# Feed-forward loads pinned in written order, cache copies in quarters, squares one group later

## The chip, the cores and the metric

The kernel runs on one core of one Trainium2 chip. The metric is the device time of one execution in microseconds (us). Three runs of the kernel before gave 2788.48, 2798.10 and 2798.96 us; their median is 2798.1 us. One more execution was profiled.

## The reference, cut to what matters

One decoder layer is applied to a prompt of 2048 tokens and to 8 single sample tokens (float32, width 1024). The part that the change touches is the feed-forward block at the end, and two caches that are shifted by one row:

```
h2 = rmsnorm(x, norm2_g)                               # (2048 + 8) x 1024
x  = x + square(relu(h2 @ w_ff1)) @ w_ff2              # w_ff1 1024 x 4096, w_ff2 4096 x 1024
y  = rmsnorm(x, final_g)
sample_win_k = concat(cache_win_k, k_new)[:, -512:]    # 8 x 512 x 6 x 64, same for v
```

The first 511 rows of each sample's new cache are rows 1 to 511 of the old one: a plain copy in DRAM.

## The kernel before, in words

Before the feed-forward block the kernel does the input projection, the windowed attention, the recurrent mixer and the output projection (up to about 1281 us). Those parts are the same in both kernels, except that a few instructions of the last output-projection blocks stand in another order.

**Stages.** The tokens go in two halves (`SB`): 1024 tokens as two blocks of 512, then 1032 tokens as two blocks of 516. For each half the 4096 hidden features are done in two quarters of 2048 (`c`), and each of these has a first layer (`ph` 1, w_ff1) and a second layer (`ph` 2, w_ff2). That makes eight stages in a row: first half c0 first layer, c0 second layer, c1 first, c1 second, then the same four for the second half.

**Seven products.** Each stage is a matrix product of 2x2 blocks done with seven block products instead of eight. `PROD_A`, `PROD_B` and `PROD_C` (just ahead of `phase_c`) say which weight blocks are added for product p, which activation blocks are added, and into which output blocks the product goes. Five of the seven need a sum of two weight blocks (tiles ax and ay), five a sum of two activation blocks (bx and by, or two hidden tiles R in a second layer). The order is 5, 1, 2, 3, 6, 4, 7 in a first layer and 5, 3, 1, 2, 6, 4, 7 in a second.

**Steps.** A product is cut into four steps, so a stage has 28. A step does 24 matmuls of 512 columns in the first half (or 24 pairs of 258 columns in the second), in groups of 12 that end in one PSUM tile pf. Float32 precision comes from splitting each operand into a high and a low part: `split` writes the high part on ScalarE (ACT: ah, bh) and the difference on VectorE (DVE: al, bl), and three matmuls use the parts. In profile rows all of these have line L74, since they go through the wrapper `Pin`, so they are told apart by tile name.

**What sets the order.** While `pinned[0]` is set, everything issued through a `Pin` wrapper (`vec`, `act`, `gpp`) keeps its written order on its engine. The DMAs of `a_load` (L1404, L1410) and `b_load` (L1439) go through plain `nc.sync`: for these the scheduler picks the order on the SP queue. SP issues in order, so a DMA that waits for its buffer holds all DMAs behind it. For step s, `ahead(s)` first writes the split of the weights of step s+2, then the splits of activation units that are due, the sum of the weights of step s+3 on GpSimd (POOL), the activation sums that are due, the load of the weights of step s+4, and the activation loads that are due. Then `run_step` writes the matmuls of step s and, group by group, the additions of pf into the output blocks (`put`: DVE, or an ACT copy where the block is new).

**Buffers.** ax has three, ay two, bx two, by one; ah, al three each, bh, bl four each. pf has six tiles of one bank in the first half and three tiles of two banks in the second.

**Squares.** In a first layer a hidden block is complete after product 3, 6, 4 or 7. Right after that put, `run_step` lets ACT do relu and square in place on the block (two instructions a group, R<-R in the profile).

**Cache copies.** `cache_copies` copies 511 rows of one sample in one DMA of 766.5 KB, DRAM to DRAM, 16 in all. The loop at the end of `phase_c` takes one at the end of each product while the first half runs. Beside that, `bg` holds jobs that fetch, finish and store rows of the result, one a step (L1302 the fetch, L1543 the transposes, L1545 to L1558 the rest).

Of the kernel before, what the change touches and what calls it, by code (L numbers as in the profile page):

```python
# [12 lines left out]
AF = mybir.ActivationFunctionType  # L13
# [3 lines left out]
P = 128  # L17
# [42 lines left out]
def body(tc, I, O):  # L60
    nc = tc.nc
# [16 lines left out]
    act = Pin(nc.scalar)  # L78
# [38 lines left out]
    h2_d = [dram.tile([D, n], F32, name=f"h2{i}_d") for i, n in enumerate((1024, 1032))]  # L117
# [500 lines left out]
    def cache_copies():  # L618
        for src, dst in (("cache_win_k", "s_k"), ("cache_win_v", "s_v")):
            sv = I[src][0].rearrange("b t h e -> b t (h e)")  # L620
            ov = O[dst][0].rearrange("b t h e -> b t (h e)")
            for b in range(NB):
                tc.keep_in_program_order(nc.sync.dma_start(ov[b, 0:511], sv[b, 1:512]))
                yield
        nc.sync.dma_start(O["s_k"][0].rearrange("b t h e -> b t (h e)")[:, 511], ks_d)
        nc.sync.dma_start(O["s_v"][0][:, 511], vs_d.rearrange("b (h e) -> b h e", e=HD + 1)[:, :, :HD])
        nc.sync.dma_start(O["s_conv"][0][:, 0:2], I["state_conv"][0][:, 1:3])
        yield
# [707 lines left out]
    def phase_c(om, o):  # L1336
# [31 lines left out]
        for sb in range(2):  # L1368
            for c in range(2):
                for ph in (1, 2):  # L1370
                    for p in ORDER[ph]:
                        dsets = ((0, 1, 2, 3),) if ph == 1 or sb == 0 else ((0, 1), (2, 3))
                        nf = 2 if len(dsets) == 1 else 4
# [3 lines left out]
                        for ds in dsets:  # L1377
                            for f0 in range(0, 8, nf):
                                bs = range(base, base + 2) if ph == 1 else range(base + f0 // 2, base + (f0 + nf) // 2)
                                for b in bs:  # L1380
# [3 lines left out]
                                                  end=False))  # L1384
# [5 lines left out]
            u_["ss"] = u_["es"] - 1  # L1390
            u_["ls"] = u_["ss"] - 1
        nb_ = dict(ls=0, ss=0, es=0)
        gpp = Pin(nc.gpsimd)

        def a_load(s):
            d = steps[s]
            blocks = PROD_A[d["p"]]
            tl = []
            for (r, q), name in zip([x for x in blocks[:2] if x], ("ax", "ay")):
                x = wst.tile([P, 4 * 256], F32, name=name, bufs=3 if name == "ax" else 2)  # L1400
                if d["ph"] == 1:
                    f0 = 2048 * d["c"] + 1024 * r + P * d["fs"][0]
                    src = w1[512 * q:512 * q + 512, f0:f0 + 256].rearrange("(k p) f -> p k f", p=P)
                    nc.sync.dma_start(x.rearrange("p (k f) -> p k f", k=4), src)  # L1404
                else:
                    nf, nd = len(d["fs"]), len(d["ds"])
                    f0 = 2048 * d["c"] + 1024 * q + P * d["fs"][0]
                    c0 = 512 * r + P * d["ds"][0]
                    src = w2[f0:f0 + P * nf, c0:c0 + P * nd].rearrange("(i p) d -> p i d", p=P)
                    nc.sync.dma_start(x.rearrange("p (i d) -> p i d", i=nf), src)  # L1410
                tl.append(x)
            d["raw"] = tl

# [15 lines left out]
        def b_load(j):  # L1429
            u_ = bunits[j]  # L1430
            W = SB[u_["sb"]][1]
            blocks = [x for x in PROD_B[u_["p"]][:2] if x]
            if u_["ph"] == 2:
                return
            u_["raw"] = []
            for (kh, th), name, nb in zip(blocks, ("bx", "by"), (2, 1)):
                x = wst.tile([P, 2, 516], F32, name=name, bufs=nb)[:, :, :W]
                r0 = 512 * kh + 256 * u_["j"]
                nc.sync.dma_start(x, h2_d[u_["sb"]][r0:r0 + 256, th * W:th * W + W].rearrange("(k p) t -> p k t", p=P))  # L1439
                u_["raw"].append(x)  # L1440

        def b_sum(j):
# [18 lines left out]
        def b_stage(s, key, f):  # L1461
            while nb_[key] < len(bunits) and bunits[nb_[key]][key] <= s:
                f(nb_[key])
                nb_[key] += 1

        def a_stage(s, f):
            if 0 <= s < len(steps):
                f(s)

        def ahead(s):  # L1470
            a_stage(s + 2, a_split)
            b_stage(s, "es", b_split)
            a_stage(s + 3, a_sum)
            b_stage(s, "ss", b_sum)
            a_stage(s + 4, a_load)
            b_stage(s, "ls", b_load)

        def put(dst, src, sign, new, nb):
            if nb > 1:
                dst = dst.rearrange("p (n w) -> p n w", n=nb)  # L1480
            if new:
                act.activation(dst, src, AF.Copy, scale=float(sign))
            else:
                vec.tensor_tensor(dst, dst, src, op=OP.add if sign > 0 else OP.subtract)

        def run_step(s, pool_, acc):
            d = steps[s]
            sb, c, ph, p = d["sb"], d["c"], d["ph"], d["p"]
            _, W, nb = SB[sb]
            w = W // nb  # L1490
            ah, al = d.pop("w")
            nf = len(d["fs"])

            def group(parts):
                pf = pool_.tile([P, nb, 512], F32, name="pf1", tag="f1")
                for i, (lh, ll, bh, bl) in enumerate(parts):
                    for x_, y_, fst, lst in ((lh, bh, i == 0, False), (lh, bl, False, False), (ll, bh, False, i + 1 == len(parts))):
                        for n in range(nb):
                            pe.matmul(pf[:, n, :w], x_, y_[:, n * w:n * w + w], start=fst, stop=lst)  # L1499
                return pf[:, :, :w] if nb > 1 else pf[:, 0, :w]  # L1500

            if ph == 1:
                av = [a.rearrange("p (k f) -> p k f", k=4) for a in (ah, al)]
                bu = [bunits[d["b0"] + j]["x"] for j in range(2)]
                for i, f in enumerate(d["fs"]):
                    fs = slice(P * i, P * i + P)
                    pf = group([(av[0][:, k, fs], av[1][:, k, fs], bu[k // 2][0][:, k % 2], bu[k // 2][1][:, k % 2])
                                for k in range(4)])
                    for blk, sign in PROD_C[p]:
                        new = (blk, f // 2, i) not in first  # L1510
                        if new and (i == 0):
                            R[blk, f // 2] = rp.tile([P, 2, 516], F32, name=f"R{blk[0]}{blk[1]}{f // 2}")
                        first[blk, f // 2, i] = True
                        cv = R[blk, f // 2][:, i, :W]
                        put(cv, pf, sign, new, nb)
                        if (blk, p) in (((0, 1), 3), ((1, 0), 4), ((1, 1), 6), ((0, 0), 7)):
                            act.activation(cv, cv, AF.Relu)
                            act.activation(cv, cv, AF.Square)
            else:
                av = [a.rearrange("p (i d) -> p i d", i=nf) for a in (ah, al)]  # L1520
                for dl, dp in enumerate(d["ds"]):
                    dsl = slice(P * dl, P * dl + P)
                    if (dp, "pf") not in d["open"]:
                        d["open"][dp, "pf"] = pool_.tile([P, nb, 512], F32, name="pf1", tag="f1")
                    pf = d["open"][dp, "pf"]
                    for i, f in enumerate(d["fs"]):
                        bh, bl = bunits[d["b0"] + f // 2]["x"]
                        bh, bl = bh[:, f % 2], bl[:, f % 2]
                        for x_, y_, a, b in ((av[0], bh, f == 0, False), (av[0], bl, False, False), (av[1], bh, False, f == 7)):
                            for n in range(nb):  # L1530
                                pe.matmul(pf[:, n, :w], x_[:, i, dsl], y_[:, n * w:n * w + w], start=a, stop=b)  # L1531
                    if d["fs"][-1] == 7:
                        pv = pf[:, :, :w] if nb > 1 else pf[:, 0, :w]
                        for blk, sign in PROD_C[p]:
                            new = (blk, dp) not in first
                            first[blk, dp] = True
                            put(acc[:, 4 * blk[0] + dp, blk[1] * W:blk[1] * W + W], pv, sign, new, nb)
# [56 lines left out]
        for s, d in enumerate(steps):  # L1594
            sb, c, ph, p = d["sb"], d["c"], d["ph"], d["p"]
            base, W, nb = SB[sb]
            new_phase = s == 0 or steps[s - 1]["ph"] != ph
# [11 lines left out]
            if ph == 2:  # L1609
                same = s and steps[s - 1]["ph"] == 2 and steps[s - 1]["p"] == p and steps[s - 1]["ds"] == d["ds"] and d["fs"][0]  # L1610
                d["open"] = steps[s - 1]["open"] if same else {}
            pinned[0] = True
            ahead(s)
            run_step(s, psf, acc)
            pinned[0] = False
            for _ in range(2 if sb and c and ph == 2 else 1):
                if bg:
                    bg.pop(0)()
            if d["end"] and sb == 0:
                next(copies, None)  # L1620
            if d["end"] and ph == 2 and c == 1:
                late = range(13, NT + 1) if sb else range(4, 8)
# [35 lines left out]
        st.close()  # L1658

    phase_c(om, o)  # L1660
    es.close()

# [26 lines left out]
```

## Time and profile before

| what | value |
|---|---|
| time, median of 3 runs | 2798.1 us (2788.48 to 2798.96) |
| the profiled execution | 2796.23 us, span 2794.5 us |
| mean granted TensorE clock | 0.960 |
| TensorE (PE) busy | 2567.7 us, 92% of the span |
| DVE, ACT, POOL busy | 64%, 41%, 35% |
| DMA issues of weights | ax x224, ay x160, 512 KB each |
| cache copies | x16, 766.5 KB each |

Durations in the rows are those of the one profiled execution. A row of the waits names the engine, line and tile that waited, what released it, the total, the number of times and the longest. A row of the stretches gives busy us and instruction counts of PE, the weight loads (PEld), DVE, ACT and POOL, then the granted TensorE clock, the share of time the DMA engines were busy, and GB/s. A row of the timeline gives start, length, engine, line, operation and count, and in brackets the idle time before it with its releaser.

### The profile page before, as it was taken

Reading aid. Unit: us, or ns where it says so; the run is one execution under the profiler, and the core shown is the slowest. Engines: PE = TensorE matmul, PEld = TensorE weight load, DVE = VectorE, ACT = ScalarE, POOL = GpSimd, SP = SyncE. Lnnn points to the kernel's source line nnn. Section 1 sums busy time; section 2 is a strip of 40 time slices with the busy share of each in tenths; the row PEclk is TensorE's granted clock in tenths of the full one; section 3 lists DMA queues with packets and bytes.
Section 4 is the critical chain, followed back from the end, with each engine's and each line's share of the span. In section 5 each row is a group of like instructions: output and inputs, shape, how many; then the busy total and the mean of one; then the engine's idle time right before and its main releaser. Section 6 shows DMA issues by size and latency. Waiting matters only on the chain. (4 is left out here: it accounts for less than half of the span.)

```text
span 2794.5 us, 41853 instructions
## 1 busy us (share of the span) xinstructions
PE 2567.7 (92%) x15646; PEld 2297.2 (82%) x15646; DVE 1790.2 (64%) x3163; ACT 1156.5 (41%) x2205; POOL 965.7 (35%) x475
## 2 busy tenths in 40 slices
PE   8999999999999889999989999898899889888886
PEld 7999999998788666777767777676799889888886
DVE  6324656664576656655768966789765576464876
ACT  5322234443454533334554355533455433355323
POOL 1000000000452342212347854466433565433662
PEclk9999999998999889999999999999999999999998
DMA  7575566655675557756656586444775444664441
GB/s 197 151 194 160 167 176 152 152 142 126 168 206 137 158 148 224 246 184 197 211 199 210 174 289 226 153 148 154 242 225 171 143 151 148 193 189 151 136 163 72
DMA packets 479536, 491.65 MB, mean 176 GB/s; under 512 B 115608, under 2 KB 406836, under 8 KB 476389
## 3 DMA queue, kind: packets, MB, share of 16 engines
q1 hardware_dynamic: 477508, 485.35, 57.8%
q0 software_dynamic: 1536, 3.10, 0.4%
q8 instruction: 123, 2.02, 0.3%
q14 instruction: 81, 0.66, 0.1%
q10 hardware_dynamic: 288, 0.53, 0.1%
HBM read 401.46 MB, written 103.59 MB: 181 GB/s over the span
## 5 line engine op out<-in xcount | busy, mean ns | idle before, releaser
L74 DVE TENSOR_TENSOR al<-ax,ah 128x1024 fp32r<-128x1024 f32 x222 | 405.2, 1825 | 342.6 <-ACT ah L74 342.3
L74 POOL TENSOR_TENSOR ax<-ax,ay 128x1024 f32<-128x1024 f32 x157 | 426.8, 2720 | 516.0 <-DMA ax<-in_w_ff_dram 295.7
L1531 PE MATMUL pf<-bl,ah 128*128 128x258 f32 (+1 forms) x1344 | 371.9, 332 | 47.2 <-DVE bl L74 47.1
L1499 PE MATMUL pf<-bh,ah 128*128 128x258 f32 (+1 forms) x1344 | 366.6, 328 | 50.2 <-DVE R L74 31.3
L1531 PE MATMUL pf<-bh,ah 128*128 128x258 f32 (+1 forms) x1344 | 365.8, 331 | 23.1 <-DVE acc L74 16.6
L74 ACT ACTIVATE ah<-ax 128x1024 fp32r<-128x1024 f32 x222 | 234.4, 1056 | 367.5 <-PE pf L1531 164.6
L1499 PE MATMUL pf<-bh,al 128*128 128x258 f32 (+1 forms) x1344 | 361.3, 326 | 11.5 <-DVE al L74 11.3
L1531 PE MATMUL pf<-bh,al 128*128 128x258 f32 (+1 forms) x1344 | 367.1, 328 | 0.0
L1499 PE MATMUL pf<-bl,ah 128*128 128x258 f32 (+1 forms) x1344 | 363.1, 325 | 1.9 <-DVE bl L74 1.9
L74 DVE TENSOR_TENSOR bl<-bx,bh 128x1032 fp32r<-128x1032 f32 (+1 forms) x134 | 284.3, 2134 | 20.6 <-ACT bh L74 19.9
L1531 PEld LDWEIGHTS pf<-bl,ah 128*128 128x128 f32 x1344 | 233.4, 198 | 73.8 <-DVE bl L74 54.6
L1499 PEld LDWEIGHTS pf<-bh,ah 128*128 128x128 f32 x1344 | 227.9, 193 | 77.1 <-DVE R L74 26.6
L74 POOL TENSOR_TENSOR bx<-R,R 128x1024 f32<-128x1024 f32 (+1 forms) x80 | 238.6, 2994 | 112.6 <-DVE bl L74 112.6
L1531 PEld LDWEIGHTS pf<-bh,ah 128*128 128x128 f32 x1344 | 231.7, 197 | 47.3 <-DVE acc L74 16.5
L1499 PEld LDWEIGHTS pf<-bh,al 128*128 128x128 f32 x1344 | 228.0, 193 | 37.0 <-DVE al L74 17.8
L163 PE MATMUL pmm<-x,wh 128*128 128x344 f32 (+1 forms) x768 | 251.5, 327 | 0.0
L164 PE MATMUL pmm<-x,wh 128*128 128x344 f32 (+1 forms) x768 | 249.5, 325 | 0.0
L165 PE MATMUL pmm<-x,wl 128*128 128x344 f32 (+1 forms) x768 | 248.9, 324 | 0.0
L1531 PEld LDWEIGHTS pf<-bh,al 128*128 128x128 f32 x1344 | 232.0, 197 | 19.8
L1499 PEld LDWEIGHTS pf<-bl,ah 128*128 128x128 f32 x1344 | 228.5, 194 | 22.0 <-DVE bl L74 2.3
L74 ACT ACTIVATE R<-R 128x512 f32<-128x512 f32 (+1 forms) x256 | 155.7, 631 | 184.8 <-DVE R L74 180.7
L1077 DVE CUSTOM_DVE_ANT_0 sm<-ps_s,nb 128x256 f32<-128x256 f32 (+1 forms) x288 | 99.9, 362 | 136.7 <-PE ps_s L1075 108.4
(467 smaller groups left out, 4909.2 us busy)
## 6 DMA issues: line engine op xcount, KB each, us to landing
ax<-in_w_ff_dram SPq DMA_DIRECT2D x224, 512.0 KB
ay<-in_w_ff_dram SPq DMA_DIRECT2D x160, 512.0 KB
xt<-in_x_prompt_dram SPq DMA_DIRECT2D x31, 512.0 KB
bx<-h_d SPq DMA_DIRECT2D x28, 516.0 KB
bx<-h_d SPq DMA_DIRECT2D x28, 512.0 KB
by<-h_d SPq DMA_DIRECT2D x20, 516.0 KB
by<-h_d SPq DMA_DIRECT2D x20, 512.0 KB
R_d<-R SPq DMA_DIRECT2D x72, 132.0 KB
```

The source lines that it names most:

```text
L74: return tc.keep_in_program_order(f(*a, **k))
L163: pe.matmul(out, lh, rh, start=first, stop=False)
L164: pe.matmul(out, lh, rl, start=False, stop=False)
L165: pe.matmul(out, ll, rh, start=False, stop=last)
L1077: vec.tensor_tensor_reduce(sm[:, :w], s_[:, e, c0:c0 + w], nb[:, o + bw - w:o + bw], 1.0, 3e38, OP.add, OP.min, mn)
L1499: pe.matmul(pf[:, n, :w], x_, y_[:, n * w:n * w + w], start=fst, stop=lst)
L1531: pe.matmul(pf[:, n, :w], x_[:, i, dsl], y_[:, n * w:n * w + w], start=a, stop=b)
```

## The change

Three things are changed, all in `phase_c` and `cache_copies`. The weight and activation loads of the feed-forward block go through a `Pin` of SP, so that they keep their written order. Each cache copy is cut into four of at most 128 rows, and one is taken at the end of every step of a second layer, not of every product of the first half. Relu and square of a group are issued after the puts of the group that follows, with a flush ahead of the first step of the next layer.

```diff
@@ cache_copies
             for b in range(NB):
-                tc.keep_in_program_order(nc.sync.dma_start(ov[b, 0:511], sv[b, 1:512]))
-                yield
+                for r in range(0, 512, 128):
+                    r1 = min(r + 128, 511)
+                    tc.keep_in_program_order(nc.sync.dma_start(ov[b, r:r1], sv[b, r + 1:r1 + 1]))
+                    yield
...
@@ phase_c
-        gpp = Pin(nc.gpsimd)
+        gpp, spq = Pin(nc.gpsimd), Pin(nc.sync)
+        late_sq = []
...
-                    nc.sync.dma_start(x.rearrange("p (k f) -> p k f", k=4), src)
+                    spq.dma_start(x.rearrange("p (k f) -> p k f", k=4), src)
...
-                    nc.sync.dma_start(x.rearrange("p (i d) -> p i d", i=nf), src)
+                    spq.dma_start(x.rearrange("p (i d) -> p i d", i=nf), src)
...
-                nc.sync.dma_start(x, h2_d[u_["sb"]][r0:r0 + 256, th * W:th * W + W].rearrange("(k p) t -> p k t", p=P))
+                spq.dma_start(x, h2_d[u_["sb"]][r0:r0 + 256, th * W:th * W + W].rearrange("(k p) t -> p k t", p=P))
...
+        def square():
+            while late_sq:
+                cv = late_sq.pop(0)
+                act.activation(cv, cv, AF.Relu)
+                act.activation(cv, cv, AF.Square)
...
+                    done = []
                     for blk, sign in PROD_C[p]:
...
                         if (blk, p) in (((0, 1), 3), ((1, 0), 4), ((1, 1), 6), ((0, 0), 7)):
-                            act.activation(cv, cv, AF.Relu)
-                            act.activation(cv, cv, AF.Square)
+                            done.append(cv)
+                    square()
+                    late_sq.extend(done)
...
             pinned[0] = True
+            if new_phase:
+                square()
             ahead(s)
...
-            if d["end"] and sb == 0:
+            if ph == 2:
                 next(copies, None)
```

On the SP queue, in the first layer of the second half's second quarter (the seventh stage), products 5 and 1, this stands before. A name's number rises in written order, so the ax and ay of one step have neighbouring numbers (ax_23038 and ay_23040).

```order
L1404 DMA ay_23040<-in_w_ff1_dram 128x4x256
L1404 DMA ax_22968<-in_w_ff1_dram 128x4x256
L1404 DMA ay_23108<-in_w_ff1_dram 128x4x256
L1404 DMA ax_23038<-in_w_ff1_dram 128x4x256
L1404 DMA ay_23172<-in_w_ff1_dram 128x4x256
L1404 DMA ax_23106<-in_w_ff1_dram 128x4x256
L1439 DMA bx_23174<-h21_d_91 128x2x516
L1404 DMA ay_23503<-in_w_ff1_dram 128x4x256
L1404 DMA ax_23170<-in_w_ff1_dram 128x4x256
```

At the same place on SP stands now:

```order
L74 DMA ax_22949<-in_w_ff1_dram 128x4x256
L74 DMA ay_22951<-in_w_ff1_dram 128x4x256
L74 DMA bx_22953<-h21_d_91 128x2x516
L74 DMA ax_23016<-in_w_ff1_dram 128x4x256
L74 DMA ay_23018<-in_w_ff1_dram 128x4x256
L74 DMA bx_23020<-h21_d_91 128x2x516
L74 DMA ax_23086<-in_w_ff1_dram 128x4x256
L74 DMA ay_23088<-in_w_ff1_dram 128x4x256
L74 DMA ax_23154<-in_w_ff1_dram 128x4x256
```

Before, the ay of the step after stood ahead of the ax of a step; now ax and ay of one step stand together, ax first. The old pattern runs from the end of the third stage on; in the first two and a half stages the rows before already stand nearly in written order.

On ACT, in the first stage, product 6 (hidden blocks R11), each row x4 is relu and square of both groups of a step:

```order
L74 ACTIVATE ah_14714<-ax_14627 128x1024
L74 ACTIVATE bh_14718<-bx_14631 128x2x512
L74 ACTIVATE R111_14206<-R111_14206 128x512 x4
L74 ACTIVATE ah_14757<-ax_14676 128x1024
L74 ACTIVATE bh_14761<-bx_14678 128x2x512
L74 ACTIVATE R112_14250<-R112_14250 128x512 x4
L74 ACTIVATE ah_14799<-ax_14723 128x1024
```

At the same place on ACT stands now:

```order
L74 ACTIVATE ah_14751<-ax_14670 128x1024
L74 ACTIVATE bh_14755<-bx_14672 128x2x512
L74 ACTIVATE R111_14205<-R111_14205 128x512 x2
L74 ACTIVATE R112_14249<-R112_14249 128x512 x2
L74 ACTIVATE ah_14793<-ax_14717 128x1024
L74 ACTIVATE R112_14249<-R112_14249 128x512 x2
L74 ACTIVATE R113_14293<-R113_14293 128x512 x2
```

The pair of a step's second group now stands behind the splits that are written with the next step; only the first group's pair stands between the puts of a step and the next ah.

On SP, in the second stage (first half, second layer), a copy stood between the loads of two products before:

```order
L623 DMA out_9_dram<-in_cache_win_v_dram 16x12264
L1410 DMA ax_15867<-in_w_ff2_dram 128x2x512
L1410 DMA ax_15907<-in_w_ff2_dram 128x2x512
L1410 DMA ax_15943<-in_w_ff2_dram 128x2x512
L1410 DMA ay_16022<-in_w_ff2_dram 128x2x512
L1410 DMA ax_15979<-in_w_ff2_dram 128x2x512
L623 DMA out_9_dram<-in_cache_win_v_dram 16x12264
```

In the same stage stands now, on SP:

```order
L625 DMA out_8_dram<-in_cache_win_k_dram 16x3072
L74 DMA ax_15784<-in_w_ff2_dram 128x2x512
L74 DMA ay_15786<-in_w_ff2_dram 128x2x512
L625 DMA out_8_dram<-in_cache_win_k_dram 16x3072
L74 DMA ax_15824<-in_w_ff2_dram 128x2x512
L74 DMA ay_15826<-in_w_ff2_dram 128x2x512
L625 DMA out_8_dram<-in_cache_win_k_dram 16x3048
```

A quarter copy stands behind the loads of a step: 28 in the second stage, 26 in the fourth, 8 in the sixth, none in the first layers; two stand ahead of the first stage. At the end of the last stage three stores of finished rows (L1558 before, L1569 now) stand ahead of all loads of the last two steps; before, the ay loads of both stood ahead of the stores, and the ax of the last but one behind the first store.

## The prediction

> **What bounds the kernel now.** I read the page first, then stretches cut at the eight stages, then the timeline of each engine where TensorE stalls.
>
> ```profile
> span 2794.5 us, 41853 instructions
> PE 2567.7 (92%) x15646; PEld 2297.2 (82%) x15646; DVE 1790.2 (64%) x3163; ACT 1156.5 (41%) x2205; POOL 965.7 (35%) x475
> ```
>
> TensorE is the bound, and what is not TensorE work shows as gaps in it. The stretches below are the eight stages in order (PE, PEld, DVE, ACT, POOL busy; clock; DMA share; GB/s).
>
> ```profile
> 1282.00:1451.00 169.00, 160.36 (x678) 126.04 (x676) 111.97 (x105) 91.20 (x135) 65.55 (x26) 0.99 0.64 215
> 1451.00:1617.00 166.00, 160.74 (x672) 128.74 (x671) 143.79 (x90) 70.60 (x81) 120.44 (x39) 0.97 0.54 184
> 1617.00:1792.00 175.00, 163.02 (x675) 129.44 (x675) 116.68 (x108) 91.17 (x129) 82.37 (x31) 0.97 0.72 237
> 1792.00:1983.00 191.00, 165.36 (x698) 131.56 (x697) 158.72 (x132) 68.48 (x82) 112.41 (x40) 0.95 0.46 153
> 1983.00:2174.00 191.00, 172.22 (x1371) 168.81 (x1370) 119.51 (x136) 101.01 (x151) 77.61 (x30) 0.98 0.67 217
> 2174.00:2363.00 189.00, 171.10 (x1321) 168.62 (x1320) 125.95 (x87) 67.92 (x77) 117.48 (x42) 0.94 0.45 145
> 2363.00:2566.00 203.00, 177.05 (x1403) 174.01 (x1402) 108.40 (x111) 99.01 (x139) 72.67 (x29) 0.97 0.57 180
> 2566.00:2775.00 209.00, 179.58 (x1386) 175.90 (x1385) 150.51 (x134) 60.31 (x70) 107.95 (x38) 0.93 0.39 127
> sum 1493.00, PE 1349.43 PEld 1203.11 DVE 1035.52 ACT 649.70 POOL 756.47; mean PE 168.68 PEld 150.39 DVE 129.44 ACT 81.21 POOL 94.56
> ```
>
> What a stage would take without stalls comes from the distance of undisturbed matmuls, one row each in the first half (23 steps of the queue between these two) and one row a pair in the second (11 between these):
>
> ```profile
> 1617.06 0.39 PE L1499 MATMUL pf<-bh,ah 128*128 128x512 f32 x1
> ...
> 1622.39 0.39 PE L1499 MATMUL pf<-bh,al 128*128 128x512 f32 x1
> ...
> 2079.76 0.40 PE L1499 MATMUL pf<-bh,ah 128*128 128x258 f32 x2
> ...
> 2082.41 0.40 PE L1499 MATMUL pf<-bh,al 128*128 128x258 f32 x2
> ```
>
> 5.33/23 is 0.232 us and 2.65/11 is 0.241 us. A stage has 28 x 24 = 672 of them: 155.7 us in the first half (a step 5.56), 161.9 in the second (a step 5.78). So the stages lose 13, 10, 19, 35 and 29, 27, 41, 47 us, 222 in all. Of that, 1493.0 - 1349.4 = 144 us is idle TensorE; the rest is transposes of finished rows and a slower clock behind stalls:
>
> ```profile
> 2414.94 0.51 PE L1499 MATMUL pf<-bh,ah 128*128 128x258 f32 x2 [2.12 <-ACT R L74]
> ...
> 2415.77 0.63 PE L1499 MATMUL pf<-bh,ah 128*128 128x258 f32 x2
> ...
> 2418.35 0.63 PE L1499 MATMUL pf<-bh,ah 128*128 128x258 f32 x2
> ```
>
> Behind a gap of 2.12 us six pairs take 2.58 us, 0.43 each for 0.24. A stall so costs more than its length, and I count losses of whole stages, not idle time. The Trainium skill ("TensorE: Matmul & The Clock Gate", section "What's actually happening") says that the clock is halved after an idle window of about 3.4 us; this gap of 2.12 was enough, so the trace does not bear the limit out. By that limit the gaps that I leave, 1 to 3 us each, would cost no clock, and of the 78 us that are not idle, about half of which my sum leaves standing, up to 39 would go as well; I go by the row.
>
> **Squares one group later.** In the stall at the end of the first stage ACT and DVE take turns:
>
> ```profile
> 1372.48 2.49 ACT L74 ACTIVATE R<-R 128x512 f32<-128x512 f32 x4 [3.70 <-DVE R L74]
> ...
> 1400.73 1.04 ACT L74 ACTIVATE ah<-ax 128x1024 fp32r<-128x1024 f32 x1
> 1403.66 2.48 ACT L74 ACTIVATE R<-R 128x512 f32<-128x512 f32 x4 [1.89 <-DVE R L74]
> ...
> 1435.49 2.49 ACT L74 ACTIVATE R<-R 128x512 f32<-128x512 f32 x4 [4.45 <-DVE R L74]
> ```
>
> ```profile
> 1401.81 1.23 DVE L74 TENSOR_TENSOR al<-ax,ah 128x1024 fp32r<-128x1024 f32 x1 [2.90 <-ACT ah L74]
> 1402.95 1.28 DVE L74 TENSOR_TENSOR R<-R,pf 128x512 f32<-128x512 f32 x2
> ```
>
> DVE cannot put a group before it has done al, al waits for ah, and ah stands behind all four square instructions of the step before. From 1372.48 to 1435.49 are nine such blocks, 7.0 us a step against 5.56 of TensorE: 1.44 x 12 steps (products 6, 4, 7) is 17 us, which is the first stage's 13 with part of the second's 10. Now two of the four (2.48/2 = 1.24 us) run while DVE does al. The chain falls to 5.76, which is nearly TensorE's own pace. That is 12 x 1.24 = 15 us a first layer, 60 for four. They cannot all come back: 5.76 is still above 5.56, and in the second half only three pf tiles lie between TensorE and the puts. I take **50**, with bounds 0 and 60. Less than nothing I exclude: no instruction is added, and the layer's last squares keep their place before the next layer's first step. Next to be late is al while POOL runs.
>
> **Loads in written order.** In the seventh stage TensorE stalls in products 5 and 1, where nothing is squared. The rows are of SP, POOL, DVE and PE:
>
> ```profile
> 2402.01 0.37 SPq L1404 DMA_DIRECT2D ay<-in_w_ff_dram  x1
> 2402.47 0.46 SPq L1404 DMA_DIRECT2D ax<-in_w_ff_dram  x1
> 2410.18 0.37 SPq L1404 DMA_DIRECT2D ay<-in_w_ff_dram  x1
> ```
>
> ```profile
> 2399.59 2.38 POOL L74 TENSOR_TENSOR ax<-ax,ay 128x1024 f32<-128x1024 f32 x1 [5.82 <-DMA ax<-in_w_ff_dram]
> 2407.77 2.38 POOL L74 TENSOR_TENSOR ax<-ax,ay 128x1024 f32<-128x1024 f32 x1 [5.79 <-issue]
> ```
>
> ```profile
> 2394.90 1.22 DVE L74 TENSOR_TENSOR al<-ax,ah 128x1024 fp32r<-128x1024 f32 x1 [3.65 <-ACT ah L74]
> ```
>
> ```profile
> 2440.03 0.80 PE L1499 MATMUL pf<-bh,ah 128*128 128x258 f32 x2 [4.55 <-DVE R L74]
> 2400.00:2450.00 50.00, 39.77 (x299) 0.93 0.54 170
> ```
>
> The ay of a later step waits for POOL's sum to end (2399.59 + 2.38 = 2401.97) and holds the ax of an earlier step, whose buffer DVE freed at 2396.1. So sum, load and sum follow each other: 8.2 us a step, against 5.78. In written order that ax goes out some 6 us sooner. Three ax buffers then turn once in 5.3 (load) + 2.4 (sum) + about 2.3 (ah, al) = 10 us per three steps, two ay buffers once in 7.7 us per two steps, under 4 us a step either way. SP's DMAs behind it (the step's copy, bx, by) are no later than now. In these 50 us 299/2 pairs were done, worth 36 us: 14 lost, and I take them back whole. The second layers show the same wait; the rows are of the second and the sixth stage, from the waits:
>
> ```profile
> POOL ax L74 <- DMA ax<-in_w_ff_dram: 0.9, 1, 0.9
> ...
> POOL ax L74 <- DMA ax<-in_w_ff_dram: 40.1, 10, 6.2
> ```
>
> The second stage, nearly in written order, has none of it and loses 10; the fourth, sixth and eighth, with the old pattern, lose 35, 27 and 47. I take 13, 12 and 5: what is left in the fourth is the row jobs, in the sixth the splits at product ends (bh and bl have buffers for one step only there), in the eighth the jobs and the store rows that now stand ahead of the last loads. The third, the fifth and the rest of the seventh give 7. Sum **51**; bounds 14 (that stretch alone) and 100 (all second layers at the level of the second stage, and the fifth and seventh halved).
>
> **Copies in quarters.** SP spends this on each:
>
> ```profile
> L623 SPq DMA_DIRECT2D out_dram<-in_cache_win_k_dram x7: 516/516/559, 1300.8 to 1473.1; - x7
> ```
>
> 48 more issues of 0.516 are 25 us, 0.4 us a step of a second layer, on a queue that stands waiting most of each step. The bytes are the same; the second stage took seven whole copies before and takes 28 quarters now. I cost it at **0**, hidden behind SP's waits; the first layers lose nine copies from a DMA share of 0.64 and 0.72, a gain I also set at 0, since the first stage runs without a gap with a copy in it:
>
> ```profile
> 1320.00:1345.00 25.00, 25.00 (x110) 1.00 0.58 186
> ```
>
> The upper bound is a rival below.
>
> The sum, against the profiled execution's own 2796.2 (its span and 1.7 around it): 2796.2 - 50 - 51 - 0 = **2695 us**. The median of the runs shown is 2 us higher, the runs spread by 10, so I leave it at that.
>
> **The rivals.** *Only the squares come back.* POOL and DVE slow each other (al is 1.23 us alone, and 144 of 166 us of DVE were busy in the second stage, with 120 of POOL), so sums may stay late without the wait on SP: 2796 - 50 = 2746. For it: the second stage has little slack left. Against: it loses only 10 so.
>
> *Only the order comes back.* ACT waits for another put in place of the one removed, and the chain stays at 7.0: 2796 - 51 = 2745. Against: the pair of the second group has al's whole time to hide in.
>
> *The quarters cost what the rest brings.* If each piece delays the loads behind it by its issue and its share of a load (192 KB at the 5.3 us of 1 MB, 1.0 us) and nothing hides it, 64 x 1.5 = 97 us: 2792, no change. Against: whole copies in the second stage left TensorE at its pace. The Trainium skill ("DMA: Bandwidth & Descriptors", section "Rules for kernel authors") advises joining small transfers and gives 0.95 us for 64 KB and 6.15 us for 1 MB; a quarter would be about 1.6 us, an estimate from these, and four of them 1.9 us more than one whole copy. No run here shows a copy's own time.
>
> *The written order makes a wait of its own, slower.* In first layers by has one buffer; its load waits for POOL's activation sum and now always holds the next step's ax and ay:
>
> ```profile
> SPq L1439 <- POOL bx L74: 87.3, 29, 7.1
> ```
>
> Forty by loads, each putting one sum and one load in line (2.4 + 5.3 against a step of 5.6: 2.1 us), cost 84 us, and the order brings nothing: 2796 - 50 + 84 = 2830. It decides from 50/40 = 1.3 us a load on. Against: the first stage has by at these places already and ran without a gap in the stretch shown.
>
> **How the numbers follow.** Both gains, 2695: 0.68, its own range 2650 to 2735. Only the squares: 0.13. Only the order: 0.08. Quarters cost the gain: 0.05. Slower by by: 0.06. A measurement of this kernel tells about 0.5%, 14 us, from no change. Faster is 0.68 + 0.13 + 0.08 = 0.89, same 0.05, slower 0.06. The range takes in the first three, 2640 to 2755, the low end from both gains at 60 and 100.
>
> **What would show it.** Right: in the first layers R<-R in pairs with an ah between them, nine blocks in about 52 us; ay and ax of a step issued together, and "POOL ax <- DMA ax" near 0 in the sixth and seventh stage; stages of about 159, 161, 161, 178, 178, 177, 173 and 204 us. Wrong: PE waits of the same sum under other names, SP rows where a copy or by goes out just ahead of late loads, or a last stage that grows by more than 5 us.

## The result and the profile after

The changed kernel takes 2687.0 us (median of 4 runs, 2685.01 to 2689.56), the kernel before beside it 2797.9 us (4 runs). The ratio is 0.961, with a 95% interval of 0.959 to 0.963: faster by 111 us. The forecast was 2695. The profiled execution took 2689.6 us, 106.7 less than that of before.

The head of the page of the changed kernel, with span and busy time of each engine:

```profile
span 2687.8 us, 41860 instructions
PE 2531.8 (94%) x15646; PEld 2277.5 (85%) x15646; DVE 1781.4 (66%) x3163; ACT 1155.6 (43%) x2205; POOL 978.7 (36%) x475
```

No engine got work taken away: DVE, ACT and POOL are busy for as long as before within 13 us. TensorE's busy time fell by 36 us without a matmul less; its mean granted clock rose from 0.960 to 0.969. The eight stages of the changed kernel, in the columns of the stretches (length, busy time of PE, PEld, DVE, ACT and POOL, clock, DMA share, GB/s):

```profile
1274.30:1433.00 158.70, 156.91 (x682) 126.53 (x681) 110.48 (x110) 95.58 (x140) 70.68 (x27) 1.00 0.68 224
1433.00:1591.70 158.70, 156.59 (x674) 125.80 (x672) 138.55 (x86) 67.24 (x76) 112.90 (x38) 1.00 0.53 181
1591.70:1754.90 163.20, 158.10 (x673) 127.88 (x672) 120.80 (x110) 95.15 (x135) 88.21 (x33) 0.98 0.74 245
1754.90:1942.50 187.60, 167.22 (x712) 133.28 (x711) 154.93 (x135) 65.09 (x77) 113.66 (x40) 0.95 0.55 185
1942.50:2120.10 177.60, 170.44 (x1370) 169.64 (x1371) 122.55 (x133) 101.59 (x150) 84.87 (x33) 0.97 0.72 237
2120.10:2300.90 180.80, 167.70 (x1347) 165.52 (x1346) 124.09 (x89) 68.07 (x77) 115.48 (x40) 0.98 0.48 155
2300.90:2463.30 162.40, 162.34 (x1345) 162.16 (x1345) 114.50 (x108) 95.48 (x134) 80.20 (x31) 1.00 0.69 228
2463.30:2666.40 203.10, 179.44 (x1396) 176.69 (x1395) 148.01 (x134) 61.64 (x72) 101.91 (x36) 0.93 0.39 128
sum 1392.10, PE 1318.74 PEld 1187.49 DVE 1033.90 ACT 649.85 POOL 767.91; mean PE 164.84 PEld 148.44 DVE 129.24 ACT 81.23 POOL 95.99
```

Cut at the first matmul of each stage, the stages of before are 169.8, 166.5, 174.5, 195.9, 189.0, 191.1, 196.2 and 209.4 us, together 1492.3 (the stretches in the prediction were cut at round times, up to 4.5 us off these places). So the stages gave back 100.2 us; another 6.4 came ahead of the first of them, which begins at 1274.31 in place of 1280.75. The seventh stage stands out: 196.2 to 162.5, with the clock at 1.00 throughout and 0.6 us over its floor of 161.9.

The squares of the first stage, ACT's rows in the timeline:

```profile
1356.26 1.30 ACT L74 ACTIVATE R<-R 128x512 f32<-128x512 f32 x2 [3.45 <-DVE R L74]
1357.47 1.05 ACT L74 ACTIVATE ah<-ax 128x1024 fp32r<-128x1024 f32 x1
1359.37 1.28 ACT L74 ACTIVATE R<-R 128x512 f32<-128x512 f32 x2
...
1408.34 1.30 ACT L74 ACTIVATE R<-R 128x512 f32<-128x512 f32 x2 [4.70 <-DVE R L74]
```

They come in pairs, with the ah of a step between them. From 1356.26 to 1408.34 are nine steps: 52.1 us, 5.79 a step on average (single steps take 4.1 to 9.1), where before it was 7.0. In the seventh stage, two of SP's rows, a stretch of 50 us and POOL's longest wait read:

```profile
2339.36 0.37 SPq L74 DMA_DIRECT2D ax<-in_w_ff_dram  x1
2339.82 0.46 SPq L74 DMA_DIRECT2D ay<-in_w_ff_dram  x1
```

```profile
2338.00:2388.00 50.00, 50.00 (x417) 50.00 (x416) 37.99 (x33) 24.52 (x34) 23.16 (x9) 1.00 0.64 212
```

```profile
POOL ax L74 <- DMA ay<-in_w_ff_dram: 45.5, 19, 6.7
```

ax and ay of a step go out together. POOL still waits for loads (45.5 us in this stage), but now for the second of a pair, and TensorE is not held up by it: it does 417 matmuls in the 50 us, where a stretch of the same length did 299 before.

### The profile page after: what moved, and what is told of

The parts are those of the page before. It is cut to its first block, busy times and chain, and to the rows that moved or that the text cites. A ratio compares the mean times of both kernels' runs of the same rounds, so it can differ in the third digit from the quotient of the medians.

```text
span 2687.8 us, 41860 instructions
## 1 busy us (share of the span) xinstructions
PE 2531.8 (94%) x15646; PEld 2277.5 (85%) x15646; DVE 1781.4 (66%) x3163; ACT 1155.6 (43%) x2205; POOL 978.7 (36%) x475
## 5 line engine op out<-in xcount | busy, mean ns | idle before, releaser
L74 POOL TENSOR_TENSOR ax<-ax,ay 128x1024 f32<-128x1024 f32 x157 | 437.0, 2785 | 387.6 <-DMA ay<-in_w_ff_dram 364.2
L74 DVE TENSOR_TENSOR al<-ax,ah 128x1024 fp32r<-128x1024 f32 x222 | 399.7, 1800 | 208.1 <-ACT ah L74 201.7
L1542 PE MATMUL pf<-bl,ah 128*128 128x258 f32 (+1 forms) x1344 | 367.5, 328 | 39.3 <-DVE bl L74 39.1
L1508 PE MATMUL pf<-bh,ah 128*128 128x258 f32 (+1 forms) x1344 | 361.3, 323 | 14.0 <-ACT R L74 6.0
L1542 PE MATMUL pf<-bh,ah 128*128 128x258 f32 (+1 forms) x1344 | 358.0, 326 | 7.6 <-ACT bh L74 5.7
L1508 PE MATMUL pf<-bl,ah 128*128 128x258 f32 (+1 forms) x1344 | 359.6, 322 | 0.0
L1542 PEld LDWEIGHTS pf<-bl,ah 128*128 128x128 f32 x1344 | 229.5, 194 | 65.3 <-DVE bl L74 46.2
L1508 PEld LDWEIGHTS pf<-bh,ah 128*128 128x128 f32 x1344 | 225.6, 191 | 35.4 <-ACT ah L74 7.6
L1542 PEld LDWEIGHTS pf<-bh,ah 128*128 128x128 f32 x1344 | 228.0, 193 | 29.7 <-ACT bh L74 6.2
L1542 PEld LDWEIGHTS pf<-bh,al 128*128 128x128 f32 x1344 | 228.6, 194 | 19.5
L1508 PEld LDWEIGHTS pf<-bl,ah 128*128 128x128 f32 x1344 | 226.0, 191 | 19.6
L1508 PEld LDWEIGHTS pf<-bh,al 128*128 128x128 f32 x1344 | 225.1, 191 | 20.4 <-DVE al L74 0.5
L74 DVE TENSOR_TENSOR R<-R,pf 128x512 f32<-128x512 f32 (+1 forms) x256 | 165.7, 682 | 69.2 <-PE pf L1508 43.1
```

The source lines that it names most:

```text
L74: return tc.keep_in_program_order(f(*a, **k))
```

## The experiments

The theory: squares and order each take away a wait of their own, the quarters do nothing, and the gains add up. The lengths of the stages in the profiled executions, each from its own first matmul to that of the next, in us:

| kernel | 1 | 2 | 3 | 4 | 5 | 6 | 7 | 8 | sum |
|---|---|---|---|---|---|---|---|---|---|
| before | 169.8 | 166.5 | 174.5 | 195.9 | 189.0 | 191.1 | 196.2 | 209.4 | 1492.3 |
| squares alone | 156.4 | 157.5 | 161.5 | 195.1 | 184.8 | 191.4 | 191.8 | 209.4 | 1447.8 |
| order alone | 167.9 | 164.8 | 169.5 | 195.4 | 184.1 | 182.1 | 178.5 | 198.4 | 1440.8 |
| quarters alone | 164.7 | 171.7 | 173.3 | 198.5 | 186.5 | 180.7 | 198.4 | 210.4 | 1484.2 |
| order and squares | 156.9 | 160.4 | 161.6 | 183.9 | 176.6 | 184.3 | 162.4 | 202.0 | 1388.1 |
| order and quarters | 168.7 | 168.0 | 172.0 | 194.0 | 187.3 | 181.4 | 174.7 | 200.6 | 1446.7 |
| changed | 158.7 | 158.7 | 163.2 | 187.6 | 177.6 | 180.7 | 162.5 | 203.1 | 1392.1 |
| ay ahead of ax | 165.4 | 178.1 | 181.7 | 207.1 | 189.5 | 203.3 | 180.3 | 225.2 | 1530.5 |
| stores on ACT | 156.6 | 161.1 | 159.8 | 188.8 | 181.5 | 182.8 | 163.5 | 202.5 | 1396.6 |
| no copies | 156.4 | 159.4 | 159.9 | 183.7 | 175.4 | 178.9 | 162.6 | 199.4 | 1375.8 |
| no row jobs, first half | 156.4 | 160.1 | 161.2 | 171.2 | 168.5 | 184.8 | 166.8 | 200.4 | 1369.5 |

**Squares alone.**

```diff
-                            act.activation(cv, cv, AF.Relu)
-                            act.activation(cv, cv, AF.Square)
+                            done.append(cv)
+                    square()
+                    late_sq.extend(done)
```

> The kernel before with the squares one group later and nothing else. Additive theory (the squares' gain and the order's stand side by side, as the prediction has it): 2798 - 50 = 2748 us, the first, third, fifth and seventh stage 10 to 15 shorter each, the second layers as before within 2. Rival, the wait is only exchanged (DVE's next wait, for ax behind the queue, takes its place): over 2780. Rival, the squares are nearly the whole gain of the change: under 2715.

2754.6 us, ratio 0.986 (0.982 to 0.990): 44 us. The first, second and third stage are at or near what the changed kernel has; the second gains because it starts when the first layer's squares are done. From the fourth on it is nearer to the kernel before; the fifth and seventh gained 4, where 10 to 15 were expected. The seventh keeps both waits of the order, POOL's for ax and TensorE's for the puts behind it.

```profile
POOL ax L74 <- DMA ax<-in_w_ff_dram: 55.1, 10, 6.6
...
PE pf L1507 <- DVE R L74: 15.7, 5, 4.9
```

**Order alone.**

```diff
-        gpp = Pin(nc.gpsimd)
+        gpp, spq = Pin(nc.gpsimd), Pin(nc.sync)
...
-                    nc.sync.dma_start(x.rearrange("p (k f) -> p k f", k=4), src)
+                    spq.dma_start(x.rearrange("p (k f) -> p k f", k=4), src)
```

> The kernel before with the feed-forward loads held in written order and nothing else. Additive theory: 2798 - 51 = 2747 us; the seventh stage about 14 to 20 shorter, the second layers 33 together, the 6 us ahead of the first stage gained here too since the loads of the first steps are part of the order; the first and third stage as before within 3. Rival, with the squares left where they were the sums are late anyway: over 2780.

2738.7 us, ratio 0.979 (0.976 to 0.983): 60 us, 51.5 of it in the stages. The third gained 5.0, where at most 3 were expected. The seventh is 17.7 shorter, and POOL no longer waits for ax there, but 11.6 us of TensorE's wait for DVE stay:

```profile
POOL ax L74 <- DMA ay<-in_w_ff_dram: 50.8, 18, 6.9
PE pf L1499 <- DVE R L74: 11.6, 5, 4.8
```

The fourth stage brings half a microsecond, although POOL's waits for ax are gone in it too. Its first 25 us show why; the row of this kernel, and the same 25 us with the squares late as well:

```profile
1768.70:1793.70 25.00, 19.16 (x68) 14.71 (x68) 19.22 (x14) 12.41 (x16) 10.38 (x4) 0.86 0.31 105
```

```profile
1745.00:1770.00 25.00, 25.00 (x109) 20.28 (x108) 19.81 (x21) 13.78 (x17) 14.04 (x6) 1.00 0.38 126
```

68 matmuls against 109, and 41 x 0.232 is 9.5 us: the second layer begins late because the squares of the third stage end late. The last of them begin 15 us into the fourth stage, after ACT has waited 6.43 us for DVE:

```profile
1783.68 2.47 ACT L74 ACTIVATE R<-R 128x512 f32<-128x512 f32 x4 [6.43 <-DVE R L74]
```

So the squares are worth more once the order is held, and the other way round.

The order also gained ahead of the first stage. Three stretches of the last output projections (301 matmuls in each kernel; those of order alone begin 12 matmuls earlier), of before and of order alone, with the first row and the sum of each:

```profile
1192.00:1217.70 25.70, 21.87 (x99) 17.62 (x98) 17.08 (x41) 6.79 (x18) 11.61 (x7) 0.93 0.92 290
...
sum 70.30, PE 64.53 PEld 51.67 DVE 39.86 ACT 21.27 POOL 13.57; mean PE 21.51 PEld 17.22 DVE 13.29 ACT 7.09 POOL 4.52
```

```profile
1181.00:1203.60 22.60, 20.37 (x98) 16.43 (x97) 15.62 (x49) 9.03 (x26) 6.81 (x5) 1.00 0.71 214
...
sum 64.30, PE 62.07 PEld 50.75 DVE 38.52 ACT 23.43 POOL 9.03; mean PE 20.69 PEld 16.92 DVE 12.84 ACT 7.81 POOL 3.01
```

6.0 us, and between exactly the same matmuls as well (70.3 and 64.3; the changed kernel has 63.3 there). Before, the scheduler drew loads of the first steps, a copy and three sums of POOL into this stretch, where order alone has one sum (POOL 13.57 against 9.03 us, DMA share 0.92 against 0.71 in its first part). Held in order, the others come at another place. Which of them cost the 6 us is not shown.

**Quarters alone, and order with squares but whole copies.**

```diff
-                tc.keep_in_program_order(nc.sync.dma_start(ov[b, 0:511], sv[b, 1:512]))
-                yield
+                for r in range(0, 512, 128):
+                    r1 = min(r + 128, 511)
+                    tc.keep_in_program_order(nc.sync.dma_start(ov[b, r:r1], sv[b, r + 1:r1 + 1]))
+                    yield
...
-            if d["end"] and sb == 0:
+            if ph == 2:
                 next(copies, None)
```

> The kernel before with the copies in quarters, issued in second layers only, and nothing else. Theory of the prediction (hidden behind SP's waits): 2798 within 6 us. Rival, the copies in the first layers did disturb (nine of them go): first and third stage 4 or more shorter each, 2785 or less. Rival, each piece costs its issue and more: second stage 7 or more longer, over 2810.

> Order and squares, copies whole and where they were. Additive theory: the time of the changed kernel, 2687 within 6 us. Rival, the quarters bring a part of the gain: over 2693, with the loss in the first and third stage. Rival, the quarters cost and are paid by the rest: under 2681.

Quarters alone: 2790.1 us, ratio 0.996 (0.995 to 0.998), a gain of 9 us, 8.1 of it in the stages. None of the three theories had it as it came: the first stage gained 5.1, the second lost 5.2, and the sixth gained 10.4, where the copies had only moved in. With the copies elsewhere the scheduler also ordered the loads anew: an ay stands ahead of an ax that is needed no later (of its own step or an earlier one) in 12, 5, 8, 5, 9, 13, 20 and 20 places of the eight stages, before in 3, 2, 5, 20, 15, 20, 20 and 20. So this run doesn't say what a quarter costs. Nor do these counts sort its stages: the fourth has 5 such places in place of 20 and is 2.6 us longer, the first 12 in place of 3 and is 5.1 shorter.

Order and squares without quarters: 2677.6 us, ratio 0.957 (0.955 to 0.960), 9 less than the changed kernel, as the rival of costly quarters had it. Additive in the main (44 + 60 = 104 against 121), with the 17 above it partly in the fourth and seventh stage: squares alone 0.8 and 4.4, order alone 0.5 and 17.7, both 12.0 and 33.8. By the stages alone the excess is 8: 44.5 + 51.5 = 96.0 against 104.2.

**The changed kernel again, and order with quarters.** No edit in the first; the second is the order and the copies of the two diffs above.

> The changed kernel itself, beside the others of this call. If the quarters cost what lies between order with squares (2677.6) and the changed kernel (2687.0): 2687 within 4 us, the ratio 0.961. If that was another chip or the build: 2680 or less.

> Order and quarters, squares where they were. If quarters cost 9 us on top of the order as they seem to on top of order and squares: 2739 + 9 = 2748. If they bring 9 as they do alone: 2730. Squares on top of order: 61 us by the pair order against order with squares; here the changed kernel less this run should be the same 61 within 8 us, and over 10 of it in the fourth stage and 12 in the seventh, where the squares alone brought 1 and 4.

2686.6 us (ratio 0.960, 0.957 to 0.963) and 2750.5 us (0.982, 0.979 to 0.986). On top of the order the quarters seem to cost 12 (2738.7 to 2750.5), with ratios whose intervals overlap; 5.9 of it lies in the stages. The squares on top of order and quarters bring 63.9, on top of the order 61.1; in the stages it is 54.6 and 52.7. Of the 54.6 the fourth has 6.4, where over 10 were expected, and the seventh 12.2.

**ay ahead of ax.** The order is held, but another one is written.

```diff
+            a_stage(s + 5, lambda k: a_load(k, "ay"))
             a_stage(s + 4, a_load)
```

(`a_load` now issues only ax, or only ay.)

> The changed kernel with its order still held, but the ay of the step after the next written ahead of the ax of the step before it. Theory (an ay whose buffer POOL frees late holds an ax whose buffer is free): the seventh stage back to 185 to 200 us from 162, the whole 25 to 50 us slower than the changed kernel, about 2712 to 2737, and POOL's waits for ax back. Rival, holding any order was the gain, not this place: within 8 us of the changed kernel.

2821.1 us, 135 more than the changed kernel measured beside it and slower than the kernel before (ratio 1.008, 1.006 to 1.011). The place is the cause, not the holding; the size was expected far too small (25 to 50), though the seventh stage, at 180.3, stays under the 185 to 200 expected of it. Only the 6 us ahead of the first stage come with any held order: between the same matmuls as above this kernel has 64.1. POOL's and SP's rows in the third stage:

```profile
1666.64 2.38 POOL L74 TENSOR_TENSOR ax<-ax,ay 128x1024 f32<-128x1024 f32 x1 [5.63 <-DMA ax<-in_w_ff_dram]
1674.60 2.38 POOL L74 TENSOR_TENSOR ax<-ax,ay 128x1024 f32<-128x1024 f32 x1 [5.58 <-DMA ax<-in_w_ff_dram]
```

```profile
1669.05 0.37 SPq L74 DMA_DIRECT2D ay<-in_w_ff_dram  x1
1669.51 0.46 SPq L74 DMA_DIRECT2D ax<-in_w_ff_dram  x1
```

A sum ends at 1669.02, at 1669.05 goes the ay, behind it the ax, 5.1 us later the next sum begins: 7.96 us a step against 5.56 of TensorE. Not every step is like this, for a whole stage loses 7 to 23 us against the changed kernel. I had taken the loss of one stage of the kernel before; but there the pattern covers only part of the steps. By the count above it stood there in 3, 2, 5, 20, 15, 20, 20 and 20 of the 20 sums of a stage; in the changed kernel it stands nowhere, and here at every sum. That accounts for the first three stages, 44.6 us. It does not account for the fourth, sixth and eighth, which are 12 to 16 us longer here than with squares alone, where the count is 20 as well, nor for the seventh, which is 11.5 shorter; why is open. The counts also sort the gains of the order on top of squares: it brings nothing in the first three stages (3, 2 and 4 places with squares alone: -0.5, -2.9, -0.1 us) and 11.2, 8.2, 7.1, 29.4 and 7.4 in the other five.

**Stores of finished rows on ACT's queue** (with order and squares, whole copies).

```diff
-            nc.sync.dma_start(O["y_prompt"][0, t0:t0 + n] if t < NT else O["y_sample"][:, 0], xt[:n])
+            nc.scalar.dma_start(O["y_prompt"][0, t0:t0 + n] if t < NT else O["y_sample"][:, 0], xt[:n])
```

> Order and squares with the stores of finished rows issued on ACT's queue in place of SP's. Theory (a store that waits for DVE on SP holds the loads of the steps behind it; fourth and eighth stage, 28 and 40 over their floors): fourth stage 8 to 15 shorter, eighth 5 to 10, in all 2655 to 2668, faster than both kernels. Rival, DVE's row work and the transposes are the loss, or ACT is held by the same wait: 2673 to 2685.

2686.6 us (ratio 0.961, 0.958 to 0.964): no gain, the fourth stage 4.9 longer than with the stores on SP. The rival was nearer, though the time is just above its range. ACT's and SP's rows at the end of the fourth stage:

```profile
1910.07 0.34 ACTq L1568 DMA_DIRECT2D out_dram<-xt  x1
1910.53 1.06 ACT L74 ACTIVATE ah<-ax 128x1024 fp32r<-128x1024 f32 x1 [7.56 <-DVE xt L1567]
```

```profile
1902.89 10.21 SPq L1302 DMA_DIRECT2D xt<-x_d  x2
1914.01 0.37 SPq L74 DMA_DIRECT2D bx<-h_d  x1
1914.44 0.45 SPq L74 DMA_DIRECT2D ax<-in_w_ff_dram  x1
```

The store now stands ahead of an ah on ACT, which comes after 7.56 us of idle time, and on SP the fetch of the next row (it needs the buffer that the store reads) holds the loads till 1914.44, 170.7 us into the stage; with the store on SP the same ax went out 168.4 us into it. The wait has moved, on both queues.

**The quarters once more, and no copies.** The changed kernel, order with squares, and the changed kernel without the 16 copies, on one chip.

```diff
                 for r in range(0, 512, 128):
-                    r1 = min(r + 128, 511)
-                    tc.keep_in_program_order(nc.sync.dma_start(ov[b, r:r1], sv[b, r + 1:r1 + 1]))
                     yield
```

> The changed kernel once more, for the comparison with order and squares on one chip: 2686 within 4 us.

> Order and squares with whole copies where they were, beside the changed kernel. If the quarters cost: 8 to 10 us under it, as the two calls apart have it, with 3 or more of it in the eight stages. If the difference is one of runs (the profiled ones differ by 8 us ahead of instruction 5700, where both kernels are the same): within 4 us of it.

> The changed kernel with the 16 cache copies left out altogether (the copied rows of the cache outputs are not written). If copies cost little in any form: within 5 us of the changed kernel. If quarters weigh on the loads: 2672 or less, the gain in the second layers.

2682.5 us (ratio 0.958, 0.956 to 0.961), 2678.3 us (0.956, 0.954 to 0.959) and 2677.3 us (0.956, 0.953 to 0.958). Whole copies are 4.2 us better than quarters, and by the whole time the two can't be told apart; the difference lies between the two theories. Without copies the time is near the theory that copies cost little. In the stages three profiles of the changed kernel have 1392.1, 1390.2 and 1395.6 us, two of order with squares 1388.1 and 1382.0, the one without copies 1375.8. By these, 16 whole copies cost about 9 us and their quarters 7 or 8 more. But profiles of one kernel differ by 5 or 6 us here, so neither size is sure, and the time as a whole shows 1 us of the 9. Some 3 us of the quarters' price have a place, the first 25 us of the first stage, in the changed kernel and in order with squares:

```profile
1264.40:1289.40 25.00, 23.27 (x99) 18.37 (x98) 10.69 (x11) 13.69 (x26) 4.42 (x2) 0.93 0.57 181
```

```profile
1272.90:1297.90 25.00, 25.00 (x114) 20.18 (x113) 14.05 (x12) 16.37 (x29) 6.74 (x2) 1.00 0.68 207
```

15 matmuls fewer are 3.5 us. In the first of the two the scheduler drew two quarters to this place, ahead of the loads of the next steps (1262.50 is SP's row here):

```profile
1262.50 0.64 SPq L625 DMA_DIRECT2D out_dram<-in_cache_win_v_dram  x1
```

The last experiment has quarters too, but none there, and its first stage is 156.4; the three profiles of the changed kernel have 158.7 to 159.9.

**No row jobs in the first half.** Rows 0 to 1023 of the prompt output are neither finished nor stored.

```diff
-            if d["end"] and ph == 2 and c == 1:
+            if d["end"] and ph == 2 and c == 1 and sb:
```

> The changed kernel with the row jobs of the first half left out (rows 0 to 1023 of the prompt output are not written). Theory (what is left over the floor in the fourth and fifth stage is the row jobs and their waits, on DVE, ACT and on SP behind stores and fetches): fourth stage 158 to 165 from 187, fifth 164 to 170 from 178 to 180, in all 2645 to 2655. Rival, POOL and DVE in each other's way are the loss (DVE 22 to 25 of 25 us before the jobs begin): fourth stage over 175.

2663.4 us (ratio 0.951, 0.949 to 0.954), 8 above the range expected. The fourth stage is 171.2, between the two theories; the fifth 168.5. The jobs cost 16 and 9 us there; the sixth and seventh are 4 longer than in the changed kernel, so the whole gained less. What is left of the fourth over its floor of 155.7 is mostly one gap. Its last stretches, TensorE at the change of halves, DVE ahead of that, and SP:

```profile
1871.00:1896.00 25.00, 24.57 (x106) 19.40 (x105) 24.12 (x16) 7.32 (x7) 20.13 (x7) 1.00 0.49 163
1896.00:1917.40 21.40, 10.77 (x48) 8.44 (x46) 11.23 (x9) 6.26 (x6) 10.42 (x5) 0.81 0.76 257
```

```profile
1906.33 0.39 PE L1542 MATMUL pf<-bh,al 128*128 128x512 f32 x1
1917.36 0.77 PE L1508 MATMUL pf<-bh,ah 128*128 128x258 f32 x2 [10.63 <-DVE acc L74]
```

```profile
1912.01 3.41 DVE L74 TENSOR_TENSOR al<-ax,ah 128x1024 fp32r<-128x1024 f32 x1 [4.78 <-ACT ah L74]
1915.34 2.47 DVE L74 TENSOR_TENSOR acc<-acc,pf 128x512 f32<-128x512 f32 x4
```

```profile
1888.63 0.44 SPq L74 DMA_DIRECT2D ay<-in_w_ff_dram  x1
1900.88 0.37 SPq L74 DMA_DIRECT2D bx<-h_d  x1
...
1902.48 0.51 SPq L74 DMA_DIRECT2D ay<-in_w_ff_dram  x1
```

TensorE has done its last matmul of the half at 1906.7, and the first of the next needs DVE's last puts, since pf gets new buffers there. The puts stand behind an al, the al waits for ah, POOL's sum and a load, and that load was issued late, at 1902.48, because the bx ahead of it waited for its buffer till 1900.88. TensorE waits for acc at the same place for 6.9 us in the changed kernel, for 7.4 with order alone and for 1.1 in the kernel before:

```profile
PE ptp L1554 <- DVE acc L74: 6.9, 1, 6.9
```

```profile
PE ptp L1543 <- DVE acc L74: 7.4, 1, 7.4
```

```profile
PE ptp L1543 <- DVE acc L74: 1.1, 2, 0.9
```

In the kernel before an ax and ay of the next half had gone out ahead of this bx, 21 us or more before the first matmul of the half; the order that is now held puts the bx first, and they go out about 15 us before it. Quarters alone, where nothing is held but the scheduler also put the bx first, has the wait too (7.7 us). No run moves this bx by itself.

## Why the prediction was right, point by point

The sum came out as worked: 101 us, of which the stages gave 100.2 between the two profiled executions. The terms were right in kind. That the sum is met within a microsecond is luck: squares and order give 104.2 together, the quarters take 4 of it back.

*The stages.* The prediction took their lengths from stretches cut at round times, 191 us for the fourth and 203 for the seventh, which are 195.9 and 196.2 from matmul to matmul. As gains, its forecast of 10, 5, 14, 13, 13, 12, 30 and 5 us stands against 11.1, 7.8, 11.3, 8.3, 11.4, 10.4, 33.7 and 6.3. As lengths, the fourth (178 forecast, 187.6 measured) and the seventh (173, 162.5) look worse than they are: about half of the one miss and two thirds of the other are the cut.

*Squares, 50.* The mechanism is the one told: pairs with ah between, 52.1 us for nine steps against about 52 forecast. That agreement tests less than it seems, since the steps vary and TensorE alone needs 50. In the stages the squares bring 44.5 alone, 52.7 on top of the order and 54.6 on top of order and quarters (44, 61 and 64 by the whole time, whose medians carry the spread of the runs). Of the 52.7, 42.5 lie in the four first layers, priced at 15 each at most, and 10.1 in the second layers: late squares also put off the start of the second layer behind them, 9.5 us in the fourth stage. Of this the prediction had named only the second stage's share.

*Order, 51.* In the stages 51.5 alone and 59.7 on top of the squares. The seventh stage was put at 14 and a part of 7; it gave 17.7 alone, about that, but 29.4 with the squares gone, since each change alone leaves the other's wait in place. The fourth was put at 13: the order gives 0.5 alone and 11.2 on top of the squares. It keeps a gap at the change of halves that I had not seen, 10.6 us in the run without row jobs, where a wait for a bx buffer holds the next weights. That is the last rival's mechanism with bx in the place of by, at one place and not forty times. The row jobs, which I named as the rest, are 16 us of the fourth stage. The upper bound of 100 was added up wrongly: its own terms (25, 17 and 37 for the second layers, 14.5 and 20.5 for the fifth and seventh) make 114. Nothing hung on it.

*Quarters, 0.* They cost 4.2 us by the whole time on one chip, which their intervals don't separate from nothing, and 7 or 8 by the stages, where profiles of one kernel differ by 5 or 6. Far from 97, but SP's waits don't seem to hide all of it. Some 3 us are the pair of quarters at the start of the first stage; the prediction priced the copies by SP's waits in the second layers alone. (Its estimate for four quarters against one whole copy comes to 1.8 us, not 1.9.)

*Not in the sum: 6 us ahead of the first stage.* I counted the last output projections at nothing because their instructions hardly change order on TensorE. The gain came with the loads and sums that stood there on SP and POOL before.

*Rivals.* Neither half alone holds the gain; each brings about half. The order alone is 6 us from its price of 2745, the squares alone 9 from 2746, so as prices of one half these were good. The wait for by cost nothing that shows in the first layers: the first stage runs at 158.7.

*The clock.* The row still speaks as in the prediction: behind the 10.63 us gap a pair takes 0.43 us (from 1917.92 to 1918.35), behind 2.12 us it did too. TensorE's busy time fell with the gaps, by 36 us.

## What to carry to other kernels

When a queue issues in order, look in its rows for a transfer that waits late and for what stands behind it: which load is written first was worth 135 us here, while holding the other order gained 6 us ahead of the stages and lost more in them. Two waits that end near each other hide each other's price, so that a change to one alone shows too little (4 and 18 us in the seventh stage, 34 together). A long gap at a change of buffers is followed back through every queue in it: here from TensorE over DVE, ACT and POOL to a small load on SP.

## What the runs showed that was not expected

DVE and POOL slow each other by about the length of a whole instruction. DVE's rows without row jobs, two with POOL's sums beside them and one without:

```profile
1880.17 3.42 DVE L74 TENSOR_TENSOR al<-ax,ah 128x1024 fp32r<-128x1024 f32 x1
1883.51 3.43 DVE L74 TENSOR_TENSOR bl<-bx,bh 128x1024 fp32r<-128x1024 f32 x1
...
1891.64 1.21 DVE L74 TENSOR_TENSOR al<-ax,ah 128x1024 fp32r<-128x1024 f32 x1
```

```profile
1882.46 3.39 POOL L74 TENSOR_TENSOR bx<-R,R 128x1024 f32<-128x1024 f32 x1
1885.81 3.38 POOL L74 TENSOR_TENSOR ax<-ax,ay 128x1024 f32<-128x1024 f32 x1
```

3.4 us is 1.2 of DVE's own and 2.2 of a POOL sum (2.4 alone), and POOL's 3.4 is 2.4 and 1.0. The lengths fit two engines that take turns, while both look busy; the rows don't show the turns themselves. That agrees with the Trainium skill ("SBUF — State Buffer", section "Who interferes with whom"), by which a DVE instruction with both inputs in SBUF contends with a GpSimd instruction that reads SBUF, and the port pair that they share is an exclusive lock. A stretch in which DVE is busy all the time is therefore no sign that DVE is the bound.

One kernel's runs differ by some 10 us from parts that no edit touches: the first stage of the changed kernel begins at 1274.3, 1266.5 and 1264.4 us in three profiled executions. For effects under 10 us the lengths of the stages are the better measure, though their sum still ranges from 1390.2 to 1395.6 us in these three.
